# The last norm of a hybrid mixer and expert block: lengths by four tiles, twelve tiles stored whole, the last experts' rows normed behind them

## The chip, the core and the metric

The kernel runs on one core of a Trainium2 chip. The core has five engines that work in parallel, each with its own queue of instructions, which it takes in order: TensorE (PE in the profile, its weight loads PEld), VectorE (DVE), ScalarE (ACT), GpSimd (POOL) and SyncE (SP). Sixteen DMA engines move data between the device's memory (HBM) and the core's SBUF; a transfer is requested by an instruction in the queue of SyncE, ScalarE or GpSimd. The metric is the device time of one execution in microseconds.

## What is computed

The reference is one residual block and a final norm, for 2048 tokens of 1024 numbers in float32. A norm, a projection and two mixers come first (a short convolution and a gated delta rule), then an output projection, then a mixture of 32 experts with two experts to a token, then the norm with which this change deals:

```python
def rms_norm(x, g):
    xf = x.astype(jnp.float32)
    y = xf * lax.rsqrt(jnp.mean(xf * xf, axis=-1, keepdims=True) + EPS)
    return (y * g.astype(jnp.float32)).astype(x.dtype)
...
        x = x + jnp.concatenate([y_a, y_b], axis=-1) @ w_out[l]
        h = rms_norm(x, ffn_norm_g[l]).reshape(Bsz * S, D)
        x = x + hier_moe(h, router_group_w[l], router_expert_w[l], w_gate[l], w_up[l], w_down[l]).reshape(Bsz, S, D)
    return rms_norm(x, final_norm_g)
```

`hier_moe` sends each token to two experts of one group of eight, and adds the two experts' outputs (SwiGLU, 1024 to 512 to 1024), each times a gate.

## The kernel before

The first 1170 us or so are mixers, output projection and router. The sum that goes into the final norm is an accumulator in HBM, `acc_d`, 2048 rows of 4 KB. The output projection writes it tile by tile (a tile is 128 tokens, there are 16).

Then the experts follow as jobs, in an order set by their number of tokens (ranks); the last three of the order, `LAST = 3`, are the ones with the fewest, with places for 120, 116 and 112 tokens (`CAPS`). A job gathers its tokens' rows, turns them (`turn`), multiplies with gate and up (`gate_up`, line 1059), then with down (`down`, lines 1094 to 1103), and an indirect DMA with an add puts the result into the rows of `acc_d` (`add`, line 1072). The weights of the job after the next are read meanwhile into staging buffers of 128 x 1024 (`stage()`, ten of them in two pools) and split into two halves of float16 by ScalarE and VectorE (lines 92 and 93).

The last norm can start before the last experts have ended, since the tokens that these three don't have need nothing more. `bix` holds, for each tile, the row numbers of its 128 tokens, and for a token of one of the last three experts a number past the end, which an indirect DMA skips. `norm_all` (lines 1362 to 1392) works through the sixteen tiles: an indirect read of the rows into a staging buffer (`load`, line 1368), the squares and their sum on ScalarE (`square`, line 1344), mean plus epsilon on VectorE (line 1345), the power of -1/2 on GpSimd (`root`, line 1348; called the root here), the product with root and gain on VectorE (`scale`, line 1351; called the gain here), and an indirect store into the output (line 1385). `AHEAD = 6` tiles are read ahead of the first square. All reads, stores and roots are in GpSimd's queue.

The tokens of the last three experts are normed by themselves, `finish` (line 1407): after an expert's sum, its rows are read from `acc_d` (`rows_of`, line 1396), which waits until that sum has landed, and then squared, rooted, multiplied and stored (`norm_chunk`, line 1404). For the last expert the rows are read before its down product, which is added to them in SBUF (`J.base`, line 1101); they are not written back to `acc_d`.

The kernel is written in Tile: its text gives the order of the instructions as a priority (`weave` takes pieces of several generators in turns; `NA` says how many pieces of the norm go into the two halves of each of the last three jobs), and a planner orders each engine's queue by priority and readiness in its own estimate of time, so it can move a ready instruction forward. It derives all waits from the tiles and tensors that are read and written; `apart` tells it that two accesses of the same tensor touch different rows, so that no wait is drawn.

After the last job stands a loop for tokens beyond an expert's places (line 1493). Its count is zero or more, and the waits for all stores stand at its entry.

Of the kernel before, what the change touches and what calls it, by code (L numbers as in the profile page):

```python
# [38 lines left out]
def hybrid_block(ctx, tc, x, mix_g, w_in, ca_w, ca_g, dn_w, a_log, dt_bias, dn_g, w_out,  # L39
# [13 lines left out]
    # ---------------------------------------------------------------- constants  # L53
# [16 lines left out]
    def weave(*parts):  # L70
        """Traces generators (generator, number of its pieces, begin, end) in turns, by begin and end in a common span."""
        live = [[b + (e - b) * 0.5 / n, (e - b) / n, g] for g, n, b, e in parts if n]
        while live:
            m = min(live, key=lambda o: o[0])
            if next(m[2], 0) == 0:
                live.remove(m)
            m[0] += m[1]
# [21 lines left out]
    # ================================================================ mixers  # L99
    with ExitStack() as ph1:  # L100
# [10 lines left out]
        # weights of beta and alpha: hi | lo  # L111
# [34 lines left out]
        def merge(main, others):  # L146
            """Traces main, 24 pieces of it, with the others spread over it; main may be None."""
# [15 lines left out]
        if True:  # L163
# [16 lines left out]
            # ---- norm of x, its halves, transposed  # L180
# [25 lines left out]
            # ---- beta, decay sums  # L206
            gates = {}

            def gate_cols(b):
# [13 lines left out]
                # sigmoid  # L223
# [5 lines left out]
                # softplus: max(z, 0) + log1p(exp(-|z|))  # L229
# [37 lines left out]
            def stage1(h, b, ws, X):  # L267
# [14 lines left out]
                # causal depthwise convolution, silu  # L282
# [12 lines left out]
                # x * sigmoid(x); beyond e^41 the sigmoid is below every float32 that matters to a sum with 1  # L295
# [14 lines left out]
            def stage2(h, b, X):  # L310
# [5 lines left out]
                # token rows of k and the lengths of k  # L316
# [14 lines left out]
                # decays, with the length of k  # L331
# [18 lines left out]
                # k k', k q'  # L350
# [12 lines left out]
                # inverses of the diagonal blocks of 16, a block to a partition  # L363
# [6 lines left out]
                # token rows of v  # L370
# [24 lines left out]
            def stage3(h, b, X):  # L395
# [4 lines left out]
                # (I - C)^-1 by doubling of the blocks; Tm: the inverse, U: its transpose  # L400
# [6 lines left out]
                # blocks of 16: only the even blocks' columns of the one, the odd blocks' of the other change  # L407
# [17 lines left out]
                # blocks of 32  # L425
# [31 lines left out]
                # the recurrence over the chunks  # L457
# [29 lines left out]
                # norm over the head (the length of q inside), gate, halves  # L487
# [28 lines left out]
            # ---- the short convolution's half  # L516
# [51 lines left out]
            # ---- the first unit: its projections start with the first tile of tokens  # L568
# [55 lines left out]
            # block numbers of row and column  # L624
# [27 lines left out]
            # selectors of the rows of the decays: row r holds part r // 16 of unit r % 16  # L652
# [37 lines left out]
            # ---- from here the space of the delta half serves the output projection  # L690
# [27 lines left out]
    # ================================================================ output projection, router  # L718
    IO = bass.IndirectOffsetOnAxis
    SYNC = mybir.DependencyInfo(mybir.DependencyClass.Sync, mybir.DependencyReason.DATA)  # L720
    NSP = 3                         # experts picked early: the ones with the fewest tokens in the first half
    NST = 2                         # of them in two passes: the first blocks' tokens, the last block's
    C1, C2 = 96, 48
    NE1 = S - TB                    # tokens of the first blocks
    # places of the picked experts, then of the others by their number of tokens
# [3 lines left out]
    LAST = 3                        # experts whose tokens are normed by themselves  # L729
# [15 lines left out]
    # expert weights: (hi, lo), row tile, column; rows of 512 or 1024; the gain of the norm is in gate and up  # L745
# [4 lines left out]
    def stage(pool=None):  # L750
        """A buffer of 128 rows of 1024; when the output projection is through there are more of them."""
# [31 lines left out]
    # router state  # L783
# [28 lines left out]
    # tokens by expert and place, less S: the sums, in SBUF, by place and rank  # L812
# [13 lines left out]
    def first_of(oh, val, shape, n):  # L826
        """oh: one-hot of the first of the zeros of val (at most 0) along the last axis."""
# [6 lines left out]
    def route(b):  # L834
# [30 lines left out]
        # places of the tokens in their experts  # L865
# [13 lines left out]
        # by expert and place (places past the last capacity only go to the blocks of the overflow)  # L879
# [10 lines left out]
        if b >= NB - 2:  # L890
            # the first experts' tokens: places below C1, C2 places from there on
# [7 lines left out]
        # gates 1 / (1 + e^d) / sum, e^d / (1 + e^d) / sum, with d = m[2] = l2 - l1  # L899
# [12 lines left out]
        if b == NB - 2:  # L912
            # the last block's tokens of the first experts stand behind the first C1 places
# [9 lines left out]
    def pick():  # L923
        """The experts with the fewest tokens in the first two blocks: fewer than C1 there, of 32 for 2048."""
# [23 lines left out]
    def entries(w, r, i, src, end, ids):  # L948
        """src: token - S, 0 where there is none."""
# [67 lines left out]
    # ---- an expert's tokens: fetched, gate and up, down  # L1017
    class Job:
        def __init__(self, key, chunks):
            self.key, self.chunks = key, chunks         # chunks: (index, index of the gate, index of the sum, width)  # L1020
            self.n = sum(c[3] for c in chunks)
            self.base = None                            # what the tokens had before
# [62 lines left out]
    def down(J):  # L1085
# [18 lines left out]
        else:  # L1104
            # columns as rows first, turned afterwards
# [35 lines left out]
    # ---- order of the work  # L1141
# [220 lines left out]
    def norm_all():  # L1362
# [15 lines left out]
        for t in range(NT + 2):  # L1378
# [3 lines left out]
            if 1 <= t <= NT:  # L1382
                xs[t - 1].root()
# [143 lines left out]
```

## Time and profile before

| | us |
|---|---|
| median of three runs | 1969.21 |
| lowest and highest run | 1964.92, 1973.45 |
| span of the profiled execution | 1978.5 |
| TensorE busy | 1774.9 (90%) |
| VectorE busy | 1407.2 (71%) |
| ScalarE busy | 1017.3 (51%) |
| GpSimd busy | 476.2 (24%) |

The shares are means over the whole span. The profiled execution took 9.3 us more than the median of the runs; all rows below are of that one execution, and their times count from the start of its span. In a line of a timeline the bracket at the end says how long the engine stood idle before the instruction and what ended that idle time.

### The profile page before, as it was taken

What the parts mean: (1) busy time and instruction counts of PE and PEld (TensorE: products, weight loads), DVE (VectorE), ACT (ScalarE), POOL (GpSimd) and SP (SyncE); (2) the same over time, 40 slices, a digit from 0 to 9 for tenths busy, and PEclk for the clock granted to TensorE, in tenths of its full rate; (3) what the DMA queues carried; (4) which work ended last, traced back from release to release, by engine and by line L of the source; (5) the groups of instructions that cost most, each with busy time, mean ns of one, the idle gap of its engine ahead of it and who ended that gap; (6) DMA issues with size and microseconds to landing.
All of it is one profiled execution on the core that took longest, in us unless ns stands there. A gap on an engine that the chain in (4) does not pass through costs nothing. (4 is left out here: it accounts for less than half of the span.)

```text
span 1978.5 us, 43091 instructions
## 1 busy us (share of the span) xinstructions
PE 1774.9 (90%) x16783; PEld 1218.3 (62%) x16783; DVE 1407.2 (71%) x2756; ACT 1017.3 (51%) x1700; POOL 476.2 (24%) x408
## 2 busy tenths in 40 slices
PE   6789999999999999999999988998889999999820
PEld 5455555555555554444454466888888999999720
DVE  8889888888888745323246748887778888888623
ACT  6654435345344323211334546776667777767522
POOL 1321211121121100000000114333222443443366
PEclk9889999999999999999999998999999999999965
DMA  4222002002001023002357858999999999999853
GB/s 141 66 67 52 10 15 51 10 16 52 9 13 45 25 66 114 27 17 59 130 173 254 294 169 269 336 312 304 290 308 362 347 334 356 341 342 299 281 162 138
DMA packets 203763, 329.25 MB, mean 166 GB/s; under 512 B 45021, under 2 KB 99366, under 8 KB 203554
## 3 DMA queue, kind: packets, MB, share of 16 engines
q1 hardware_dynamic: 177010, 264.90, 39.9%
q0 software_dynamic: 22016, 52.48, 10.3%
q10 hardware_dynamic: 4528, 9.06, 1.2%
q8 instruction: 133, 2.18, 0.5%
q14 instruction: 76, 0.62, 0.1%
HBM read 276.21 MB, written 54.53 MB: 167 GB/s over the span
## 5 line engine op out<-in xcount | busy, mean ns | idle before, releaser
L134 PE MATMUL acc<-hT,whl 128*128 128x512 f16 x2640 | 635.0, 381 | 0.2 <-DVE hT L203 0.2
L1059 PE MATMUL a<-xT,wgu 128*128 128x136 f16 (+19 forms) x6528 | 407.7, 225 | 22.8 <-DVE sl L1066 13.7
L1059 PEld LDWEIGHTS <-wgu 128*128 128x128 f16 x6528 | 399.3, 100 | 30.4 <-issue 25.9
L134 PEld LDWEIGHTS <-whl 128*128 128x128 f16 x2640 | 253.0, 99 | 248.2 <-issue 11.2
L93 DVE SCALAR_TENSOR_TENSOR wgu<-mst,gw,wgu 128x1024 f16<-128x1024 f32 x256 | 317.2, 1277 | 15.8 <-ACT wgu L92 15.8
L92 ACT ACTIVATE wgu<-mst,gw 128x1024 f16<-128x1024 f32 x256 | 279.0, 1138 | 31.3 <-DMA mst<-in_w_up_dram 28.2
L979 PE MATMUL a<-wo,yb 128*128 128x512 f16 x768 | 178.0, 384 | 0.0
L1072 POOL DMA_INDIRECT acc_d<-yo,tabS x53 | 106.0, 1999 | 257.1 <-ACT yo L1120 200.3
L93 DVE SCALAR_TENSOR_TENSOR wd<-mst,wd 128x1024 f16<-128x1024 f32 x128 | 154.5, 1215 | 6.2 <-ACT wd L92 6.2
L1129 PE MATMUL a<-ac,wd 128*128 128x136 f16 (+12 forms) x1920 | 142.8, 230 | 2.7 <-issue 1.2
L92 ACT ACTIVATE wd<-mst 128x1024 f16<-128x1024 f32 x128 | 130.7, 1045 | 19.4 <-DMA mst<-in_w_down_dram 17.3
L1129 PEld LDWEIGHTS <-wd 128*128 128x128 f16 x1920 | 130.2, 98 | 5.7 <-issue 3.9
L979 PEld LDWEIGHTS <-yb 128*128 128x128 f16 x768 | 72.5, 99 | 80.5 <-issue 5.4
L294 DVE SCALAR_TENSOR_TENSOR cv<-raw,pcol,cv 128x512 f32<-128x512 f32 x144 | 114.9, 800 | 1.6
L1028 POOL DMA_INDIRECT xr<-h_d,tabG x54 | 69.5, 1286 | 171.7 <-PE t L1044 161.8
L1066 DVE SCALAR_TENSOR_TENSOR sl<-a,sl 128x136 f32<-128x136 f32 (+19 forms) x136 | 39.6, 293 | 91.4 <-ACT sl L1065 80.5
L1065 ACT ACTIVATE sl<-a 128x136 f32<-128x136 f32 (+19 forms) x136 | 37.1, 275 | 123.9 <-PE a L1059 101.4
L1094 PE MATMUL pl<-wd,ac 128*120 128x512 f16 (+6 forms) x336 | 80.4, 384 | 0.7 <-ACT ac L92 0.7
L382 DVE TENSOR_TENSOR pr<-Ts,fs 32x1 f32<-32x1 f32 (+14 forms) x240 | 76.6, 319 | 4.0 <-DMA fs<-dscr 0.3
L1116 PE MATMUL pl<-id,yt 128*128 128x128 f32 (+13 forms) x320 | 55.4, 293 | 25.4 <-ACT yo L1120 19.5
L1033 POOL DMA_INDIRECT gs<-gt_d,gix x54 | 74.0, 1371 | 16.4 <-issue 16.0
L545 ACT ACTIVATE osq<-acv 128x512 f32<-128x512 f32 x16 | 10.1, 628 | 125.5 <-DVE acv L543 125.5
(351 smaller groups left out, 2592.3 us busy)
## 6 DMA issues: line engine op xcount, KB each, us to landing
mst<-in_w_gate_dram SPq DMA_DIRECT2D x256, 256.0 KB
mst<-in_w_up_dram SPq DMA_DIRECT2D x256, 256.0 KB
mst<-in_w_down_dram SPq DMA_DIRECT2D x128, 512.0 KB
wst<-in_w_in_dram SPq DMA_DIRECT2D x28, 512.0 KB
xt<-in_x_dram SPq DMA_DIRECT2D x16, 512.0 KB
ydr<-yh SPq DMA_DIRECT2D x64, 128.0 KB
x<-in_x_dram SPq DMA_DIRECT2D x16, 512.0 KB
yb<-ydr SPq DMA_DIRECT2D x16, 512.0 KB
```

The costliest lines, as they stand in the source:

```text
L92: A.activation(hi, src, AF.Copy, scale=scale)
L93: (eng or V).scalar_tensor_tensor(lo, src, scale, hi, op0=OP.mult, op1=OP.subtract)
L134: T.matmul(acc, w[:, i, k, :], hT[b][:, j, k, :], start=(n == 0), stop=(n == 3 * KT - 1))
L294: V.scalar_tensor_tensor(y, tap(j), pcol[:, q:q + 1], y, op0=OP.mult, op1=OP.add)
L382: V.tensor_tensor(q, Ts[:, 0:i, 0:i].rearrange("p j m -> p m j"), bc(fs[:, None, 0:i, i], [32, i, i]), op=OP.mult)
L979: T.matmul(po, yb[:, i, k, c * P:(c + 1) * P], wo[:, j, k, n * FF:(n + 1) * FF], start=(q == 0), stop=(q == 3 * KT - 1))
L1028: G.indirect_dma_start(out=xr[0:cw].rearrange("p a k c -> p (a k c)"), out_offset=None, in_=h2_d[0:end, :], in_offset=IO(ap=ix, axis=0))
L1033: G.indirect_dma_start(out=g[0:cw], out_offset=None, in_=gt_d[0:end * NE, :], in_offset=IO(ap=gx, axis=0))
L1059: T.matmul(pg[:, q, 0:n], wq[:, i, k, q, f * P:(f + 1) * P], xT[:, j, k, 0:n], start=(z == 0), stop=(z == 3 * KT - 1))
L1072: st = G.indirect_dma_start(out=acc_d, out_offset=IO(ap=sx, axis=0), in_=yo[0:cw], in_offset=None, bounds_check=S - 1, oob_is_err=False, c ...
L1094: T.matmul(py[0:n], ac[:, i, k, 0:n], wd[:, j, k, q * FF:(q + 1) * FF], start=(z == 0), stop=(z == 3 * FF // P - 1))
L1129: T.matmul(pg[:, u, 0:n], wd[:, i, k, d * P:(d + 1) * P], ac[:, j, k, 0:n], start=(z == 0), stop=(z == 3 * FF // P - 1))
```

## The change

Three things change, all behind line 1332.

The norm of the tiles goes by groups of four. Four squares write their sums into four columns of one tile, one instruction on VectorE and one root on GpSimd do the four columns, and four gains follow, each with its store behind it. `AHEAD` is 8, and `NA` spreads the pieces anew.

The stores of tiles 0 to 11 (`NPL = 12`) are plain DMAs of 128 whole rows on SyncE's queue. They also write rows of the last experts' tokens, whose contents in the staging buffer are left over from before; these rows are stored again later. Tiles 12 to 15 keep the indirect store that skips them.

The last experts' rows are read once, in the last job: after the sums of the two experts before have landed, three indirect reads get the rows of the last expert (`J.base`) and of the two before (`ends`, into buffers of the pool `o1`). The two are normed and stored behind the store of tile 12; the last expert's rows are written to `acc_d` by an indirect DMA (in `finish`), normed into another buffer and stored at the end. The indirect stores are declared apart from one another where their rows differ, the plain stores from none of them.

The rest of the diff takes out comments and is left out here.

```diff
@@ -1332,32 +1332,28 @@
             for _ in g:
                 pass
 
-    class Norm:
-        def __init__(self, xf, n):
-            self.x, self.n = xf[0:n], n
-        def square(self):
-            self.s = o2.tile([P, 1], F32, name="ss4", bufs=6)[0:self.n]
-            jk = m2.tile([P, D], F16, name="jk", tag="yt")
-            A.activation(jk[0:self.n], self.x, AF.Square, accum_out=self.s)
-            V.tensor_scalar(self.s, self.s, 1.0 / D, EPS, op0=OP.mult, op1=OP.add)
-        def root(self):
-            G.tensor_tensor(self.s, self.s, mhalf[0:self.n, 0:1], op=OP.pow)
-        def scale(self):
-            V.scalar_tensor_tensor(self.x, self.x, self.s, gfin[0:self.n], op0=OP.mult, op1=OP.mult)
-    AHEAD = 6
+    AHEAD = 8
     LP, WE = 0, 0.6
-    NA = ((0, 3), (6, 6), (9, 9))
+    NA = ((0, 4), (12, 10), (10, 10))
+    GT = 4
+    NPL = NT - GT
     loads, stores, adds, outs = [], [], [], []
 
     def apart(st, others):
         for o in others:
             tc.declare_no_dep(st.ins, o.ins, reason="rows of other tokens")
+    def square(x, s, n=P):
+        jk = m2.tile([P, D], F16, name="jk", tag="yt")
+        A.activation(jk[0:n], x, AF.Square, accum_out=s)
+    def root(s):
+        V.tensor_scalar(s, s, 1.0 / D, EPS, op0=OP.mult, op1=OP.add)
+        G.tensor_tensor(s, s, mhalf[0:s.shape[0], 0:s.shape[1]], op=OP.pow)
+    def gain(x, s, n=P, dst=None):
+        V.scalar_tensor_tensor(x if dst is None else dst, x, s, gfin[0:n], op0=OP.mult, op1=OP.mult)
 
     def norm_all():
         xs = {}
@@ -1375,52 +1371,70 @@
         for t in range(AHEAD):
             load(t)
             yield 1
-        for t in range(NT + 2):
-            if t < NT:
-                xs[t] = Norm(xs[t], P)
-                xs[t].square()
-            if 1 <= t <= NT:
-                xs[t - 1].root()
-            if t >= 2:
-                st = G.indirect_dma_start(out=out2, out_offset=IO(ap=bix[:, t - 2:t - 1], axis=0), in_=xs.pop(t - 2).x,
-                                          in_offset=None, bounds_check=S - 1, oob_is_err=False)
-                apart(st, outs + stores)
-                stores.append(st)
-                load(t - 2 + AHEAD)
-            if 1 <= t <= NT:
-                xs[t - 1].scale()
+        for t0 in range(0, NT, GT):
+            s = o2.tile([P, GT], F32, name="ss4")
+            for i in range(GT):
+                square(xs[t0 + i], s[:, i:i + 1])
+                yield 1
+            root(s)
+            for i in range(GT):
+                t = t0 + i
+                x = xs.pop(t)
+                gain(x, s[:, i:i + 1])
+                if t < NPL:
+                    nc.sync.dma_start(out2[t * P:(t + 1) * P, :], x)
+                else:
+                    st = G.indirect_dma_start(out=out2, out_offset=IO(ap=bix[:, t:t + 1], axis=0), in_=x,
+                                              in_offset=None, bounds_check=S - 1, oob_is_err=False)
+                    apart(st, outs + stores)
+                    stores.append(st)
+                load(t + AHEAD)
+                yield 1
+    def rows_of(ix, cw, xf):
+        G.indirect_dma_start(out=xf[0:cw], out_offset=None, in_=acc_d, in_offset=IO(ap=ix, axis=0))
+        return xf[0:cw]
+    def norm_rows(x, dst=None):
+        n = x.shape[0]
+        s = o2.tile([P, 1], F32, name="ss1", bufs=4)[0:n]
+        square(x, s, n)
+        root(s)
+        gain(x, s, n, dst)
+    def store_rows(x, sx, more=True):
+        st = G.indirect_dma_start(out=out2, out_offset=IO(ap=sx, axis=0), in_=x, in_offset=None,
+                                  bounds_check=S - 1, oob_is_err=False)
+        if more:
+            apart(st, stores)
+            outs.append(st)
+    def finish(J):
+        if J.base:
+            ix, gx, sx, cw = J.chunks[0]
+            st = G.indirect_dma_start(out=acc_d, out_offset=IO(ap=sx, axis=0), in_=J.base[0][0:cw], in_offset=None,
+                                      bounds_check=S - 1, oob_is_err=False)
+        else:
+            st = add(J)[0]
+        apart(st, loads)
+        adds.append(st)
+        yield 1
+    def last_rows(na, ends):
+        for _ in na:
+            if len(stores) == 1 and not outs:
+                for x, sx in ends:
+                    norm_rows(x)
+                for x, sx in ends:
+                    store_rows(x, sx)
             yield 1
 
-    def rows_of(ix, cw):
-        xf = stage()
-        G.indirect_dma_start(out=xf[0:cw], out_offset=None, in_=acc_d, in_offset=IO(ap=ix, axis=0))
-        return xf
-    def norm_chunk(xf, sx, cw):
-        N = Norm(xf, cw)
-        N.square()
-        N.root()
-        N.scale()
-        return G.indirect_dma_start(out=out2, out_offset=IO(ap=sx, axis=0), in_=xf[0:cw], in_offset=None,
-                                    bounds_check=S - 1, oob_is_err=False)
-    def finish(J):
-        ix, gx, sx, cw = J.chunks[0]
-        if not J.base:
-            st = add(J)[0]
-            apart(st, loads)
-            adds.append(st)
-            yield 1
-        st = norm_chunk(J.base[0] if J.base else rows_of(ix, cw), sx, cw)
-        apart(st, stores)
-        outs.append(st)
-        yield 1
     eids = {}
 
     def part(j, i):
         if j < NST or j >= len(jobs):
             return
         r = jobs[j].key
@@ -1471,7 +1485,10 @@
         if left <= LAST:
             n1, n2 = NA[LAST - left]
             if left == 1:
-                J.base = [rows_of(J.chunks[0][0], J.n)]
+                J.base = [rows_of(J.chunks[0][0], J.n, stage())]
+                ends = [(rows_of(L.chunks[0][0], L.n, o1.tile([P, D], F32, name="end", tag="hh")), L.chunks[0][2])
+                        for L in jobs[-LAST:-1]]
+                na = last_rows(na, ends)
             parts.append((slices(na, n1), n1, 0, 1))
         weave(*parts)
         parts = [(prio(part(j + 2, 0), PW if j == 0 else 0), 4, 0, 1) if left != 3 else (seq(*(part(j + 2, i) for i in range(3))), 12, 0, WE)]
@@ -1487,8 +1504,11 @@
             parts.append((slices(na, n2), n2, WE if left == 3 else 0, 1))
         weave(*parts)
     drain(na)
+    end = stage()[0:J.n]
+    norm_rows(J.base[0][0:J.n], end)
+    store_rows(end, J.chunks[0][2])
     nb_ = nc.values_load(nblk[0:1, 0:1], min_val=0, max_val=NB2)
     with tc.For_i(0, nb_, 1) as i:
         overflow()
@@ -1498,7 +1518,9 @@
         J = Job("o", [(ox[:, 1:2], ox[:, 2:3], ox[:, 0:1], P)])
         drain(fetch(J), load_expert("o", e), turn(J), gate_up(J), down(J))
         add(J)
-        norm_chunk(rows_of(ox[:, 1:2], P), ox[:, 0:1], P)
+        x = rows_of(ox[:, 1:2], P, stage())
+        norm_rows(x)
+        store_rows(x, ox[:, 0:1], False)
 
 
 # ---- launch: one core; inputs and outputs as the reference has them ----
```

## Rows read from the trace of the kernel before

**Rows 1.** Windows by stretch of 1850 to 1980: PE, PEld, DVE, ACT, POOL, clock, DMA share, GB/s.

```profile
1850.00:1900.00 50.00, 34.99 (x488) 30.17 (x486) 28.30 (x47) 26.81 (x49) 33.37 (x22) 0.87 0.64 211
1900.00:1950.00 50.00, 6.36 (x35) 3.71 (x32) 11.75 (x20) 9.27 (x20) 30.57 (x25) 0.60 0.51 153
1950.00:1980.00 30.00, 0.00 (x0) 0.00 (x0) 8.00 (x9) 3.18 (x6) 14.91 (x13) 0.50 0.33 120
```

**Rows 2.** Timelines of PE and ACT: start, us, line, operation, count, idle before, releaser.

```profile
1896.34 4.63 PE L1059 MATMUL a<-xT,wgu 128*128 128x112 f16 x48 [11.46 <-DVE sl L1066]
...
1903.56 3.44 PE L1094 MATMUL pl<-wd,ac 128*112 128x512 f16 x15 [0.65 <-ACT ac L92]
...
1880.85 1.06 ACT L1344 ACTIVATE jk<-mst 120x1024 f16<-120x1024 f32 x1 [9.25 <-DMA mst<-acc_d,tabG]
...
1930.50 1.06 ACT L1344 ACTIVATE jk<-mst 116x1024 f16<-116x1024 f32 x1 [26.99 <-DMA mst<-acc_d,tabG]
```

**Rows 3.** Timeline of POOL, 1857 to 1967: reads, stores, roots of the last norm.

```profile
1857.51 1.86 POOL L1368 DMA_INDIRECT mst<-acc_d,bix  x1 [12.42 <-DMA mst<-in_w_down_dram]
...
1862.29 6.33 POOL L1368 DMA_INDIRECT mst<-acc_d,bix  x1 [0.57 <-DVE wgu L93]
...
1885.04 2.07 POOL L1368 DMA_INDIRECT mst<-acc_d,bix  x1 [0.18 <-issue]
...
1889.25 2.04 POOL L1385 DMA_INDIRECT out_dram<-mst,bix  x1 [0.18 <-issue]
...
1905.54 2.15 POOL L1072 DMA_INDIRECT acc_d<-yo,tabS  x1 [0.30 <-issue]
...
1920.36 1.30 POOL L1396 DMA_INDIRECT mst<-acc_d,tabG  x1 [8.48 <-DMA acc_d<-yo,tabS]
...
1923.30 1.04 POOL L1368 DMA_INDIRECT mst<-acc_d,bix  x1 [0.30 <-issue]
...
1931.99 0.57 POOL L1348 TENSOR_TENSOR ss<-ss,mhalf 116x1 f32<-116x1 f32 x1 [6.41 <-DVE ss L1345]
...
1966.91 0.99 POOL L1404 DMA_INDIRECT out_dram<-mst,tabS  x1 [1.61 <-DVEq L1493]
```

**Rows 4.** Windows of the tail, columns as in group 1 (DMA share, then GB/s, last).

```profile
1866.00:1869.00 3.00, 1.00 (x20) 1.00 (x20) 3.00 (x8) 0.55 (x3) 2.69 (x2) 1.00 0.00 0
...
1869.00:1887.00 18.00, 14.54 (x200) 11.86 (x198) 4.64 (x13) 7.22 (x15) 11.68 (x10) 1.00 0.72 203
...
1872.00:1884.00 12.00, 10.66 (x148) 8.68 (x147) 1.08 (x3) 3.15 (x7) 6.25 (x7) 1.00 0.88 260
...
1869.00:1971.00 102.00, 24.56 (x272) 19.23 (x269) 30.74 (x54) 24.41 (x52) 68.76 (x56) 0.64 0.53 168
...
1971.00:1978.50 7.50, 0.00 (x0) 0.00 (x0) 0.00 (x0) 0.00 (x0) 0.00 (x0) 0.50 0.00 0
```

**Rows 5.** Groups by shape, 1840 to 1980: count, busy us, mean ns, idle before, releasers.

```profile
L1385 POOL DMA_INDIRECT out_dram<-mst,bix x16 | 29.4, 1836 | 3.3 <-issue 3.3
...
L1351 DVE SCALAR_TENSOR_TENSOR mst<-mst,ss,gfin 128x1024 f32<-128x1024 f32 x16 | 20.6, 1285 | 23.6 <-POOL ss L1348 20.8 <-DMA mst<-acc_d,bix 2.8
L1344 ACT ACTIVATE jk<-mst 128x1024 f16<-128x1024 f32 x16 | 16.7, 1044 | 13.3 <-DMA mst<-acc_d,bix 13.3
L1348 POOL TENSOR_TENSOR ss<-ss,mhalf 128x1 f32<-128x1 f32 x16 | 12.8, 800 | 1.3 <-DVE ss L1345 0.9
...
L1072 POOL DMA_INDIRECT acc_d<-yo,tabS x4 | 6.7, 1684 | 15.6 <-ACT yo L1120 14.7 <-issue 0.9
```

**Rows 6.** Timelines of SyncE's queue and of DVE, same columns as group 2.

```profile
1856.07 0.33 SPq L775 DMA_DIRECT2D mst<-in_w_down_dram  x1
...
1863.13 4.62 DVE L93 SCALAR_TENSOR_TENSOR wd<-mst,wd 128x1024 f16<-128x1024 f32 x4
...
1889.10 1.29 DVE L1351 SCALAR_TENSOR_TENSOR mst<-mst,ss,gfin 128x1024 f32<-128x1024 f32 x1 [2.75 <-POOL ss L1348]
```

**Rows 7.** DMA queues, 1840 to 1980: packets, MB, share of 16 engines.

```profile
q0 software_dynamic: 6912, 18.46, 42.6%
```

## Prediction: what the change does to the time

> **What bounds the kernel now.** I read the windows of the last 130 us first, then the timeline of TensorE and ScalarE, then GpSimd's timeline, then the groups of instructions by shape, and last the transfers. The windows show that the change lies in a tail of its own: from 1850 on TensorE's busy time falls from 35.0 us in a stretch of 50 to 6.4 and then to nothing, while GpSimd is busy 33.4, 30.6 and 14.9 us [rows 1]. The last matmul ends at 1903.56 + 3.44 = 1907.0 [rows 2], and the span ends 71.5 us later. What runs there is the last norm: sixteen reads of a tile, sixteen norms, sixteen stores, and a read, norm and store for each of the last three experts.
>
> GpSimd paces it. It issues every read and every store and computes every root, in a queue that goes in order. From the first tile store at 1889.25 to the last store at 1966.91 [rows 3] it alternates root and store with hardly an idle moment, except for two holes. The first is 8.48 us ahead of the read at 1920.36, which waits for the sum of expert 30 to land; that sum was issued at 1905.54, took 2.15, and landed 12.7 us after. The second is 6.41 us ahead of the root at 1931.99, which waits for those rows to be squared [rows 3]. ScalarE stood 26.99 us for these rows, with tiles behind it in its queue [rows 2]. The transfer engines are no limit on average: share 0.53 and 168 GB/s from 1869 to 1971; then nothing moves, and 7.5 us of closing follow [rows 4].
>
> **The change, part by part.** The profiled execution has a span of 1978.5 us; the median of the runs is 1969.2, so a result on the span is multiplied by 0.995 at the end.
>
> Twelve stores leave GpSimd. One is 1.836 us, with 3.3 / 16 = 0.21 us of issue around it [rows 5]: 12 x 2.04 = 24.5 us. They become plain stores on SyncE's queue, which has no weights left to ask for by then. Issue there is 0.33 us in the nearest row, the last weight request [rows 6], hidden beside the gain that makes the next tile (1.285 us, [rows 5]); without that cover it would be 12 x 0.33 = 4 us.
>
> Sixteen roots of one column become four of four columns. One takes 0.800 us [rows 5]. A root of four columns has no row; it lies between 0.8 (nothing for width) and 3.2 (four times). I take 0.8, because the cost of a root in these rows follows the instruction, not its one column per partition: 12 x 0.8 = 9.6 us off GpSimd, or 0 at the other end. The twelve small products on VectorE that go with them are free, since VectorE is busy only 30.7 of 102 us [rows 4].
>
> The group has a price at its start: the first gain waits for four squares in place of one, 3 x 1.04 = 3.1 us [rows 5]. It also has a credit: the first square no longer stands behind the rows of expert 29 in ScalarE's queue (that square came at 1880.85 [rows 2], while tile reads had been issued from 1857.5 on [rows 3]). I put the two together at 0, between -5 and +3.
>
> The second hole goes, 6.4 us: the rows of experts 29 and 30 are now read together with the last one's and squared behind the tiles, when they have long landed. The first hole stays, at another place: the three reads still wait for the sum of expert 30, and what is queued behind them on GpSimd (the roots of the later groups, the reads of the last tiles) waits too. Eight tiles read ahead in place of six give that wait more work in front of it. I leave it at its price of now.
>
> Added on GpSimd: one write of the last expert's sum into the accumulator, 1.684 us as the other writes there [rows 5] plus 0.3 issue, 2.0 us; nothing if the engine waits for something else then, 4 us if it waits for the reads before it.
>
> A new wait: the scattered stores of tiles 12 to 15 and those of the last experts' rows write the same output as the twelve plain stores and are not declared apart from them, so the store of tile 12 waits for the landing of the store of tile 11. Behind it on GpSimd stand the roots and stores of the last experts' rows, the stores of tiles 13 to 15, the write and the last norm. From below its price is 3.1 us: the last store's issue ends at 1967.9 and transfers are over by 1971 [rows 3, 4]. From above it is the 12.7 us of the sum that landed behind a backlog. I take 5, near the first, because the plain stores do not queue behind reads on GpSimd's queue.
>
> Sum on GpSimd: -24.5 - 9.6 - 6.4 + 2.0 + 5.0 = -33.5 us; with all terms at their worse ends (-24.5 + 4 - 0 - 6.4 + 4 + 12.7 + 3) it is -7, with all at their better ends (-24.5 - 9.6 - 6.4 + 0 + 3.1 - 5) -42.
>
> **What is late next: the transfers.** From 1869 to 1971 they moved 102 us x 168 GB/s = 17.1 MB in 0.53 x 102 = 54 us of full use [rows 4]. Whole tiles carry the last experts' rows too (120 + 116 + 112 = 348 rows of 2048, twelve sixteenths of it, 4 KB each: 1.1 MB), and the new write is 0.46 MB; 18.6 MB then, of a software queue that moved 18.46 MB in the tail [rows 7], or 59 us of full use. Starting at 1869 that ends at 1928 at a share of 1, at 1936 at the share of 0.88 that the engines reach while reads stand in line (1872 to 1884), at 1951 at the 0.72 of 1869 to 1887, which has an idle stretch in it [rows 4]. GpSimd's sum would need 1971 - 33.5 = 1937.5, so a share of 0.86 throughout, and the new landing waits speak against that. I take 0.78, between the two rows: 59 / 0.78 = 75.6 us, to 1944.6, which is 26.4 us earlier. Closing stays at 7.5. Span 1952, and in terms of the median 1969.2 - 26.3 = 1943.
>
> [...]
>
> **The rivals.**
> First, VectorE holds GpSimd up in bursts. A store that runs while a gain runs takes 2.04 us (1889.25, with the gain at 1889.10), a read with no gain beside it 1.04 (1923.30) [rows 3, 6]. Under four conversions of weights back to back (4.62 us from 1863.13) one read took 6.33, and no byte moved from 1866 to 1869 [rows 3, 4, 6]. Four gains back to back are 4 x 1.285 = 5.1 us; if each of the four bursts holds the queue as a whole, 20.5 us of the sum go: -33.5 + 20.5 = -13, time 1956. For it: that one read. Against: reads from 1857.5 on went through under conversions too, the first at 1.86 [rows 3]. [...]
>
> Second, the reading of the last rows gets in the way. If the planner puts these three reads ahead of the root of the third group, that group and the fourth wait for a landing of 12.7 us and for three reads of 1.3 us [rows 3]: -26.4 + 12.7 + 4 = -9.7, time 1959.6. Then the change does not do what it says, "behind the tiles". For it: the reads come first in the text of the last job. Against: eight tiles ahead, and the planner has lifted ready reads before (nine tile reads, from 1857.51 to 1885.04, before the first tile store [rows 3]).
>
> Third, slower: the transfers keep the pace of now, because each is started by the landing of another. 18.6 MB at 168 GB/s are 110.7 us, to 1979.7 instead of 1971: +8.7, time 1978. It decides from a mean pace under 18.6 / 102 = 182 GB/s. For it: plain and scattered stores would share the engines and waits for landings are added. Against: 260 GB/s from 1872 to 1884 and gaps without any transfer that are GpSimd's doing [rows 4].
>
> Fourth, better: the transfers come near full use and all terms to their better ends, -40: 1929.
>
> **How the numbers follow.** Forecast 1943 (its own range 1935 to 1952) 0.60; bursts, 1956, 0.16; reads in the way, 1960, 0.08; slower, 1978, 0.08; better, 1929, 0.08. Half a per cent, 10 us, is about what a measurement of this kernel tells from no change. Faster by more: 0.58 + 0.14 + 0.02 + 0.08, some 0.80 with the tails; within: 0.12; slower: 0.08. The range 1928 to 1962 leaves out the slower case and the half of the better one, and the ends of the others, 0.17 in all.
>
> **What would show it right or wrong.** Right: GpSimd with 4 scattered tile stores, 4 wide roots under 1 us, no hole of 6 us ahead of a root; SyncE with 12 stores; transfers at a share near 0.78 from 1869 on, over by 1945. The wait before tile 12's store shows the price of the landing. Bursts: reads of over 4 us beside four gains. Reads in the way: GpSimd idle over 8 us at a read of the accumulator with roots behind it. Wrong altogether: TensorE's last matmul later than 1907, because products of the last expert stand behind four gains on VectorE; it stood 11.46 us for VectorE now [rows 2]. That would hit the last norm, which needs the last expert's product.

## The result and the profile after

The changed kernel takes 1949.2 us as the median, the kernel before 1971.0 in the same comparison: a ratio of 0.9892, interval 0.9868 to 0.9915, or 21 us less. The forecast was 1943 with a range of 1928 to 1962, so the direction and roughly the size are right; why they are is another matter, since several terms of the sum and the step on the transfers were wrong, and their errors partly cancel.

The two profiled executions have spans of 1978.5 and 1946.2 us, 32 us apart. Eleven of these lie ahead of the tail, where the change has nothing: the first tile read starts at 1857.51 before [rows 3] and at 1846.74 after. From that read to the end it is 121.0 us before and 99.5 after, 21.5 less, and this agrees with the medians. All stages below are counted from the first tile read of the same execution.

GpSimd's timeline of the kernel after, with the columns as before (start, duration, operation, idle time before it and its releaser), shows the stages:

```profile
1846.74 1.87 POOL L1364 DMA_INDIRECT mst<-acc_d,bix  x1 [12.36 <-DMA mst<-in_w_down_dram]
...
1884.35 2.14 POOL L1072 DMA_INDIRECT acc_d<-yo,tabS  x1 [1.69 <-ACT yo L1103]
...
1900.55 0.94 POOL L1395 DMA_INDIRECT mst<-acc_d,tabG  x1 [11.39 <-issue]
1901.79 1.00 POOL L1395 DMA_INDIRECT end<-acc_d,tabG  x1 [0.30 <-issue]
1903.10 1.25 POOL L1395 DMA_INDIRECT end<-acc_d,tabG  x1 [0.30 <-issue]
1904.36 2.04 POOL L1353 TENSOR_TENSOR ss<-ss,mhalf 128x4 f32<-128x4 f32 x2
1911.92 0.56 POOL L1353 TENSOR_TENSOR ss<-ss,mhalf 120x1 f32<-120x1 f32 x1 [5.52 <-DVE ss L1352]
1915.29 1.55 POOL L1353 TENSOR_TENSOR ss<-ss,mhalf 116x1 f32<-116x1 f32 x1 [2.81 <-DVE ss L1352]
1918.74 1.05 POOL L1387 DMA_INDIRECT out_dram<-mst,bix  x1 [1.90 <-SPq L1513]
...
1925.55 1.29 POOL L1406 DMA_INDIRECT out_dram<-end,tabS  x1 [0.84 <-DMA out_dram<-end,tabS]
...
1935.20 0.98 POOL L1406 DMA_INDIRECT out_dram<-mst,tabS  x1 [5.21 <-DMA out_dram<-end,tabS]
```

The unbroken row of roots and stores of [rows 3] is gone: 4 stores of tiles are left on this queue, and they come at the very end. What the reader is to see instead is idle time. The longest stands ahead of the three reads at 1900.55: they wait for the sum of expert 30, issued at 1884.35 (the profile names no releaser on this line; in the runs "half" and "later" below it names that sum on the same read). Behind them stand the roots of the third and fourth group (1904.36); the third group's squares were done by 1886.8. Two more idle stretches, 5.52 and 2.81 us, stand ahead of the roots of the last experts' rows (1911.92 and 1915.29). The last store waits 5.21 us for the landing of the store of expert 30's rows, issued at 1925.55.

The windows of the kernel after (PE, PEld, DVE, ACT, POOL, clock, DMA share, GB/s) show the same from the side of the transfers, to be read beside [rows 4]:

```profile
1875.00:1887.00 12.00, 9.84 (x176) 8.94 (x173) 5.41 (x8) 6.24 (x13) 8.13 (x7) 1.00 1.01 388
...
1893.00:1902.00 9.00, 1.93 (x8) 0.87 (x6) 0.06 (x1) 1.09 (x3) 1.15 (x2) 0.88 0.18 49
...
1858.20:1939.20 81.00, 28.15 (x273) 19.23 (x269) 29.06 (x43) 22.94 (x50) 39.04 (x33) 0.70 0.69 227
...
1939.00:1946.20 7.20, 0.00 (x0) 0.00 (x0) 0.00 (x0) 0.00 (x0) 0.00 (x0) 0.50 0.00 1
```

While reads and plain stores overlap, the engines are full at 388 GB/s. Then, for nine microseconds in which GpSimd waits for one sum, they run at a share of 0.18.

### The profile page after: what moved, and what is told of

It is laid out like the page before. It is cut to its first block, busy times and chain, and to the rows that moved or that the text cites. A ratio compares the mean times of both kernels' runs of the same rounds, so it can differ in the third digit from the quotient of the medians.

```text
span 1946.2 us, 43064 instructions
## 1 busy us (share of the span) xinstructions
PE 1771.7 (91%) x16783; PEld 1211.5 (62%) x16783; DVE 1406.6 (72%) x2744; ACT 1017.4 (52%) x1700; POOL 448.7 (23%) x385
## 5 line engine op out<-in xcount | busy, mean ns | idle before, releaser
L134 PEld LDWEIGHTS <-whl 128*128 128x128 f16 x2640 | 253.2, 99 | 249.8 <-issue 13.3
L1059 PE MATMUL a<-xT,wgu 128*128 128x136 f16 (+19 forms) x6528 | 396.8, 223 | 3.1 <-DVE sl L1066 2.2
L1059 PEld LDWEIGHTS <-wgu 128*128 128x128 f16 x6528 | 390.5, 98 | 8.6 <-issue 4.1
L1094 PE MATMUL pl<-wd,ac 128*120 128x512 f16 (+6 forms) x336 | 87.0, 406 | 21.5 <-ACT ac L92 21.5
```

What stands on the lines that cost most here:

```text
L134: T.matmul(acc, w[:, i, k, :], hT[b][:, j, k, :], start=(n == 0), stop=(n == 3 * KT - 1))
L1059: T.matmul(pg[:, q, 0:n], wq[:, i, k, q, f * P:(f + 1) * P], xT[:, j, k, 0:n], start=(z == 0), stop=(z == 3 * KT - 1))
L1094: T.matmul(py[0:n], ac[:, i, k, 0:n], wd[:, j, k, q * FF:(q + 1) * FF], start=(z == 0), stop=(z == 3 * FF // P - 1))
```

## The experiments

I cut the tail into three stages with marks that every kernel has: from the first tile read to the issue of expert 30's sum; from there to the first read of the last experts' rows, which waits for its landing; from there to the end. The middle stage is the landing itself only where the profile names it as what ended the wait; in "scatter", "cap120" and "scatter120" it names something else, and in the changed kernel and "groupsonly" nothing, so there it is an upper bound. Times in us, of one profiled execution each; the ratio to the kernel before with its interval comes from timed rounds.

| kernel | to the sum | landing | rest | tail | ratio to before |
|---|---|---|---|---|---|
| before | 48.0 | 14.8 | 58.1 | 121.0 | 1 |
| changed | 37.6 | 16.2 | 45.7 | 99.5 | 0.9892 (0.9868 to 0.9915) |
| scatter | 44.3 | 16.3 | 51.7 | 112.3 | 0.9946 (0.9930 to 0.9961) |
| rowsonly | 51.5 | 15.2 | 48.0 | 114.6 | 0.9946 (0.9927 to 0.9965) |
| groupsonly | 52.3 | 15.2 | 49.2 | 116.7 | 0.9969 (0.9956 to 0.9983) |
| half | 35.7 | 17.1 | 43.8 | 96.6 | 0.9889 (0.9868 to 0.9911) |
| later | 37.6 | 14.6 | 44.7 | 96.9 | 0.9890 (0.9869 to 0.9911) |
| latesq | 30.0 | 15.3 | 56.9 | 102.2 | 0.9912 (0.9891 to 0.9932) |
| before120 | 48.7 | 6.8 | 54.4 | 109.9 | 0.9905 (0.9888 to 0.9922) |
| cap120 | 36.4 | 9.9 | 39.4 | 85.7 | 0.9795 (0.9774 to 0.9816) |
| cap117 | 37.0 | 10.3 | 40.1 | 87.4 | 0.9805 (0.9783 to 0.9828) |
| scatter120 | 45.9 | 9.5 | 45.3 | 100.7 | 0.9882 (0.9857 to 0.9907) |
| capall | 37.0 | 10.5 | 41.2 | 88.7 | 0.9704 (0.9682 to 0.9726) |
| best | 36.6 | 9.8 | 44.8 | 91.2 | 0.9730 (0.9709 to 0.9751) |

**The parts of the change.** My theory was that GpSimd's queue sets the tail; the rival, that the transfers do. First, the changed kernel with all stores given back to GpSimd ("scatter"):

```diff
-    NPL = NT - GT
+    NPL = 0
...
-            if len(stores) == 1 and not outs:
+            if len(stores) == NT - GT + 1 and not outs:
```

> The changed kernel with all sixteen tiles stored by indirect DMAs from GpSimd (none by SyncE); groups of four and the late reading of the last rows stay. If GpSimd's queue sets the tail: twelve stores of 2.04 us come back to it, 24.5 us, less the 1.9 to 5 us of waiting for plain stores to land that goes; some of it can fall into the 11.4 us in which the queue stands for the sum of expert 30. So 8 to 20 us more than the changed kernel's 1949, 1957 to 1969, and over 95 us from the first tile read to the end becoming 108 to 119. If transfers set it: 1.1 MB fewer, 3 to 5 us less, 1944 to 1946.

Measured: 0.9946 / 0.9892 is 0.55% or 10.7 us more than the changed kernel (1959.9 against 1949.2). The direction is the queue's, against the transfers, which would have gained; the size is at the lower end of what the queue let one expect. The run does not separate the time of the stores in the queue from what their landings hold up: in "scatter" the wait ahead of the three reads ends with the landing of a scattered store.

Then also a root for each tile ("rowsonly"), so that the late reading of the last rows is left, together with the eight tiles read ahead and the new spread of the pieces (`AHEAD`, `NA`), which stay in every run made from the changed kernel:

```diff
-        for t0 in range(0, NT, GT):
-            s = o2.tile([P, GT], F32, name="ss4")
-            for i in range(GT):
+        for t0 in range(0, NT, 1):
+            s = o2.tile([P, GT], F32, name="ss4", bufs=6)
+            for i in range(1):
                 square(xs[t0 + i], s[:, i:i + 1])
                 yield 1
-            root(s)
-            for i in range(GT):
+            root(s[:, 0:1])
+            for i in range(1):
```

> The late reading of the last experts' rows alone: all tiles stored from GpSimd, a root for each tile. If GpSimd's queue sets the tail: as the run with scattered stores, plus twelve roots of 0.8 us, 9.6 us, less 3 us for the first gain that waits for one square in place of four: 1964 to 1976, that is within 0.3% of the kernel before. If the removed hole ahead of the last experts' root (6.4 us) is a gain by itself, 1964. If transfers set it: 1946 to 1949.

Measured: the same 0.9946 as "scatter". That is 1960 us, a little under what the theory and the rival of the removed hole gave and far above what the transfers gave. The roots in groups are worth nothing here that the intervals (3 to 4 us to either side) could tell, and the late reading with `AHEAD` and `NA` is worth 10.6 us; no run has those two alone, so what they give by themselves is not shown. GpSimd's groups by shape of these two kernels, 1840 to the end, say what the groups did on the queue (count, busy us, mean ns); rowsonly first, then scatter:

```profile
L1387 POOL DMA_INDIRECT out_dram<-mst,bix x16 | 17.1, 1067 | 8.0 <-issue 3.8 <-DVE ac L93 3.6 <-DVE mst L1356 0.3
L1353 POOL TENSOR_TENSOR ss<-ss,mhalf 128x1 f32<-128x1 f32 x16 | 12.1, 762 | 1.7 <-DVE ss L1352 1.5
```

```profile
L1387 POOL DMA_INDIRECT out_dram<-mst,bix x16 | 24.3, 1522 | 9.8 <-DVE mst L1356 6.5 <-issue 2.6 <-DVE ss L1352 0.3
...
L1353 POOL TENSOR_TENSOR ss<-ss,mhalf 128x4 f32<-128x4 f32 x4 | 4.2, 1043 | 0.1
```

Four wide roots take 4.2 us where sixteen took 12.1: 8 us less. But the stores cost 7.2 us more in total, and the saving is gone. One store shows it best, in GpSimd's timeline of "scatter":

```profile
1915.61 5.41 POOL L1387 DMA_INDIRECT out_dram<-mst,bix  x1 [2.20 <-DVE mst L1356]
```

Beside it, in VectorE's timeline of the same kernel, stand the gains:

```profile
1914.04 6.06 DVE L1356 SCALAR_TENSOR_TENSOR mst<-mst,ss,gfin 128x1024 f32<-128x1024 f32 x5
```

The store's 5.41 us end at 1921.0, just behind the five gains, which end at 1920.1; the next store takes 0.99. This is the rival of the bursts, and it is real, but it is shown only where a store stands in GpSimd's queue beside them. The plain stores of the changed kernel don't: their twelve requests on SyncE's queue take 0.33 us in the median and 0.81 at most, and the four behind the start of a burst of five gains (1905.72 to 1911.78) 0.33 to 0.64.

The groups without the late reading ("groupsonly", with all stores on GpSimd) keep the last experts' rows behind each sum:

```diff
...
+        x = J.base[0][0:cw] if J.base else rows_of(ix, cw, stage())
+        norm_rows(x)
+        store_rows(x, sx)
+        yield 1
...
-                na = last_rows(na, ends)
...
-    end = stage()[0:J.n]
-    norm_rows(J.base[0][0:J.n], end)
-    store_rows(end, J.chunks[0][2])
```

> The groups of four alone (with eight tiles read ahead): all tiles stored from GpSimd, the last experts' rows read, normed and stored behind each expert's sum as before. If GpSimd's queue sets the tail: 9.6 us of roots less than the kernel before, 3 us more for four squares at the start: 1961 to 1968. If the order on ScalarE sets it (its squares wait for rows with the experts' products behind them): 1968 to 1975, no gain or a loss, since more squares stand ahead.

Measured: 0.9969, 6.1 us less than before (1964.5 in its median), as the queue let one expect. So the gains of the parts seem to depend on what else is there: groups, again with `AHEAD` and `NA`, 6 us by themselves and nothing to be told from noise on top of the late reading.

**The bytes.** The plain stores with half of their columns ("half"):

```diff
-                    nc.sync.dma_start(out2[t * P:(t + 1) * P, :], x)
+                    nc.sync.dma_start(out2[t * P:(t + 1) * P, 0:D // 2], x[:, 0:D // 2])
```

> The changed kernel, but each plain store of tiles 0 to 11 writes only the first 512 of 1024 columns (the other half of these rows is left out): 3.1 MB less to transfer, the same number of instructions. If transfers set the tail: 3.1 MB at the 227 GB/s of the tail are 13.8 us less, 1935. If the queues and single landings set it: the landing of the last plain store and of reads beside stores comes 1 to 4 us sooner, 1945 to 1949.

Measured: 0.9889 against 0.9892, no difference, though 3.1 MB less moved. The sum of expert 30 lands as late as ever, as GpSimd's timeline of "half" says:

```profile
1899.38 0.95 POOL L1395 DMA_INDIRECT mst<-acc_d,tabG  x1 [12.32 <-DMA acc_d<-yo,tabS]
```

So the transfers do not set the tail by what they carry, and the step of the prediction that let them do so falls.

**The order.** Two edits ask what stands in the way of what. "later" makes the three reads of the last job after the first half of its work instead of ahead of it:

```diff
-            if left == 1:
-                J.base = [rows_of(J.chunks[0][0], J.n, stage())]
...
         weave(*parts)
+        if left == 1:
+            J.base = [rows_of(J.chunks[0][0], J.n, stage())]
...
```

> The changed kernel with the three reads of the last experts' rows moved behind the first half of the last job, so that the root of the third group stands ahead of them in GpSimd's queue (that of the fourth still behind). If the reads in the way of the roots cost time: the third group's gains and plain stores go at 1887 in place of 1906 and the store of tile 12 no longer waits for them: 4 to 8 us less, 1941 to 1945. If the sum of expert 30 sets the tail whatever stands behind it: 1947 to 1950.

Measured: 0.9890, no difference. The third group's root now comes ahead of the reads, 15 us sooner counted from the first tile read, and the end does not move: the landing still ends the wait. "latesq" moves squares behind expert 30's products:

```diff
-    NA = ((0, 4), (12, 10), (10, 10))
+    NA = ((0, 4), (4, 18), (10, 10))
```

> The changed kernel with eight pieces of the tiles' norm moved from the first half of the last job but one to its second half (4 and 18 pieces in place of 12 and 10), so that fewer squares stand ahead of expert 30's products on ScalarE. If ScalarE's squares, which wait for rows, hold up expert 30's sum: that sum is issued 5 to 10 us sooner than 1884 (counted from the first tile read: 28 to 33 us in place of 37.6) and the time falls by 4 to 8 us. If GpSimd or the landing sets it: 1947 to 1955, with the tiles' stores later.

Measured: the sum of expert 30 is issued 7.6 us sooner (30.0 for 37.6), as expected if ScalarE's squares hold it up, but the time does not fall: 0.9912. What was gained ahead of the sum is lost behind it (56.9 for 45.7). The tiles' own squares come later (the last of them at 1914.65, 64.4 us from the first tile read, and in the changed kernel at 1902.11, 55.4 us), which fits the second expectation.

**The landing.** In every kernel so far the sum of expert 30 took 14.6 to 17.1 us from issue to landing, whether half the bytes were moved beside it or not; the sum of expert 29 took 6.7 in the kernel before (issued at 1868.92, the read behind it at 1875.61). One has 116 rows, the other 120, and the share of 0.18 in the last nine microseconds is that of about 3 engines out of 16 (0.18 x 16 = 2.9); in the kernel before it is 0.20 from 1917.0 to the read at 1920.36. The new theory, an estimate from such shares, was that the transfer of 116 rows runs on some 4 engines and one of 120 rows on more; the rival, that it stands in line. "cap120" gives that expert four places more:

```diff
-            132, 132, 128, 128, 124, 124, 124, 120, 120, 120, 116, 112]
+            132, 132, 128, 128, 124, 124, 124, 120, 120, 120, 120, 112]
```

> The changed kernel with 120 places in place of 116 for the last expert but one (expert 30 of the order), so that its sum, its reads and its stores are transfers of 120 rows. [...] Then the sum of expert 30 lands in 6 to 9 us, its rows in 6 in place of 10.8, and the time falls by 8 to 14 us to 1935 to 1941. Rival: the sum lands late because it stands behind reads and stores in line; 120 rows change nothing, 1947 to 1951, and the wait stays at 15 us or more.

Measured: 1927.9 and 0.9795, 19 to 21 us less than the changed kernel, more than the theory asked for. GpSimd's timeline of "cap120":

```profile
1815.77 0.96 POOL L1028 DMA_INDIRECT xr<-h_d,tabG  x1 [5.80 <-PE t L1044]
...
1840.49 1.87 POOL L1364 DMA_INDIRECT mst<-acc_d,bix  x1 [8.98 <-DMA mst<-in_w_gate_dram]
...
1876.90 1.65 POOL L1072 DMA_INDIRECT acc_d<-yo,tabS  x1 [0.65 <-ACT yo L1103]
...
1886.80 0.93 POOL L1395 DMA_INDIRECT mst<-acc_d,tabG  x1 [5.62 <-DVE ac L93]
...
1915.43 0.98 POOL L1406 DMA_INDIRECT out_dram<-mst,tabS  x1 [1.61 <-DVE mst L1356]
```

The landing takes 9.9 us in place of 16.2, the last store waits 1.61 for its gain and no longer for a store of 116 rows, and the tail is 13.8 us shorter. Another 7.5 lie just ahead of it: from the gather of expert 30's tokens (1815.77) to the first tile read it is 24.7 us here and 32.2 after (from 1814.51; the gather itself came 1.3 us later here). It is so in the others too: 31.3 in the kernel before, 24.7 to 25.0 in "before120", "cap117" and "capall". ScalarE waits for weights there in the changed kernel (3.56 us at 1823.15) and hardly at all in "cap120". That would fit a gather of 116 rows that is slow as well, with weights waiting behind it; but the engines are full in both stretches (shares 1.01 and 1.04), and no run separates this, so the cause of these 7.5 us stays open.

The same edit in the kernel before ("before120"):

> The kernel before with 120 places in place of 116 for expert 30. If 116 rows run on 4 engines: the hole of 8.5 us ahead of the read and that of 6.4 us ahead of the root of expert 30's rows shrink by 5 to 8 and 2 to 4 us: 7 to 11 us less, 1960 to 1964. Rival, backlog: no change, 1967 to 1973.

Measured: 0.9905, 19 us less, where 7 to 11 were expected; the landing is 6.8 us in place of 14.8, and the tail is 11.1 us shorter. The rest lies ahead of the tail, for which the expectation had no term. To tell the number 116 itself from what else came with four places more, one place more ("cap117"). Were it the number itself, nearly all of what 120 places gave was due, 1927 to 1934; were it something else, 1940 to 1950:

> The changed kernel with 117 places in place of 116 for expert 30. [...]

Measured: 0.9805, within the interval of 120 places, with a landing of 10.3 us. One row more makes the kernel 17 us faster, so it is not that fewer rows are moved; what sets 116 apart from 117 and 120 no run shows. The windows of the last 8 us ahead of the read, "cap117" first and then "cap120", stand against the share of 0.18 above:

```profile
1889.77:1897.77 8.00, 3.98 (x11) 1.92 (x12) 1.43 (x6) 3.38 (x11) 1.68 (x3) 0.79 0.87 287
```

```profile
1878.60:1886.80 8.20, 2.93 (x7) 1.56 (x8) 1.44 (x6) 4.30 (x11) 2.04 (x2) 0.63 0.93 300
```

Their shares are 0.87 and 0.93, or some 14 and 15 engines of 16 (0.87 x 16 = 13.9). The packets of the changed kernel's trace fit its 0.18: from 1892.7 to its read 2 to 6 are under way at once, mostly 3 or 4. So the slow landing is that of a transfer of which few packets move at a time, with two tile reads finishing beside it. The profile does not name the engines one by one, so on how many of them each of the three transfers ran is not shown.

With the landing out of the way, what are the plain stores worth ("scatter120": scatter with 120 places)?

> All tiles stored from GpSimd, as in the run with scattered stores, with 120 places for expert 30. That run lost 10.7 us against the changed kernel. If part of its stores lay in the hole in which GpSimd waits for the sum of expert 30 (11.4 us with 116 places, 5.6 with 120): the loss grows to 13 to 18 us, 1941 to 1946. If the stores' own price is what was lost (1.0 to 1.5 us each where no gain runs beside them, in place of 2.0): the loss stays at 9 to 12, 1937 to 1940.

Measured: 0.9882 / 0.9795, 0.9% or 17 us more than "cap120", where it was 10.7 with 116 places. Both have an interval of 5 to 7 us to either side, so that the loss grew is not shown. Nor do the stages show stores that had lain in the hole ahead of the three reads: two stand there in either kernel (1893.64 and 1896.34 in "scatter", 1893.89 and 1896.56 in "scatter120"), and the tails differ by 15.0 us here and by 12.8 with 116 places.

Three experts in the middle have 124 places, so their gathers and sums are transfers of 124 rows. "capall" gives them 128, and expert 30 the 120 of "cap120":

```diff
-            132, 132, 128, 128, 124, 124, 124, 120, 120, 120, 116, 112]
+            132, 132, 128, 128, 128, 128, 128, 120, 120, 120, 120, 112]
```

> [...] If such a transfer takes 5 to 8 us from a stretch in which the engines are full with weights, as the gather of 116 rows did (7.5 us from its issue to the first tile read): 10 to 24 us less than with 120 alone (1928), 1904 to 1918. If only the tail is touched by it: 1926 to 1930.

Measured: 0.9704, another 0.9% or 18 us, and the tail is no shorter than with 120 alone (88.7 us and 85.7). It is gained among the weights: from one gather of tokens (1315.61 in "cap120", 1323.95 in "capall") to the thirteenth behind it (1533.13 and 1519.42) it is 22 us shorter. What a single transfer of 124 rows takes of this is not shown. This version beats both kernels, by 3.0% and 1.9%. "later" on top of it is "best":

> The last with the three reads of the last experts' rows behind the third group's root. If the reads stand in the way only as long as the sum of expert 30 lands late: no change to the last, within 3 us. If the third group's 5 us of gains and the landing of its stores were the next to be late: 3 to 6 us less than the last.

Measured: 0.9730, and so neither of the two expectations. In the same rounds the lowest of five runs of "best" (1924.5) lies above the highest of five of "capall" (1922.9), a loss of 7 us between the medians. In the profiled executions 4.7 of this stand ahead of the first gather of an expert's tokens, where the edit does nothing (1127.22 and 1122.54), and 2.5 in the tail; the cause is not shown.

## Why the prediction was right or wrong

Split by the three stages, the 21.5 us of the tail are 10.4 up to the sum of expert 30 (48.0 to 37.6), -1.4 in its landing, and 12.5 behind it (58.1 to 45.7).

*GpSimd paces the tail*: half right. Giving the queue its stores back costs 10.7 us and halving the bytes nothing, so for the stores it is the queue, or what waits in it, and not the bytes that the change relieved. But the longest single wait was for a landing, which the prediction saw as the "first hole" and let stand at its price.

*Twelve stores, -24.5*: mis-sized. They are worth 10.7 us on top of the rest, and 17 by the medians of the kernels with a short landing. The reading of 1.836 us was that of stores beside gains [rows 5]; sixteen stores in "rowsonly" took 1.067 each. And a part of the time that they leave in the queue stands idle: ahead of the roots of the last experts' rows GpSimd waits 5.52 and 2.81 us in the kernel after, while in "scatter" stores fill the queue up to these roots.

*Roots, -9.6*: the four-column root takes 1.05 us, near the lower bound, as chosen. Between "rowsonly" and "scatter" GpSimd saved 8 us in roots and spent 7 more in stores, and the time gained nothing that can be told from noise. That the bursts of gains which come with the groups hold up stores is shown for the store of 5.41 us; for the rest of the 7 us it is argued.

*The second hole, -6.4, the write, +2.0*: the late reading with `AHEAD` and `NA` gave 10.6, more than the 4.4 of these two terms. Its third stage is 10 us shorter than before (48.0 for 58.1) and its first 3.5 longer, and nothing in the runs splits that further. In the changed kernel the hole did not go. The rows were to be squared when they had long landed; they are read only at 1901.79 and 1903.10, behind the sum of expert 30, ScalarE waits 4.41 and 4.9 us for them, and 5.52 and 2.81 us stand ahead of their roots.

*The first hole stays*: it grew, from 8.48 [rows 3] to 11.39 us, with the roots of two groups behind it. That is the second rival, which I gave 0.08 and a time of 1960. It happened, and for the third group it cost nothing: with its root ahead of the reads ("later") the time is the same. The fourth group's root could hardly have come sooner: of its tile reads, one issued by 1888.16 landed only at 1900.9, about when the sum of expert 30 did, and its last square ended at 1903.2.

*The new wait, +5*: the store of tile 12 waited 1.90 us, less than the lower bound, since the queue stood for expert 30's rows until shortly before. Another wait had no term: the last store behind the landing of the store of expert 30's rows, 5.21 us, of which 3.9 come after its gain was done (1931.30); the kernel with 120 places waits 1.61 us there, for the gain alone.

*The transfers are late next, share 0.78*: the step that failed. 18.4 MB moved (81.0 us x 227 GB/s; 18.6 were estimated), at a share of 0.69 and not 0.78, so that they were over 81 us after the mark instead of 75.6. The share was low because requests waited for landings, not because the engines were at a limit, and "half" shows that bytes do not count. What stood in the place of the bytes was the landing of one sum of 116 rows at a share of 0.18, worth 13.8 us of the tail in "cap120", for which the prediction had only the 8.48 us of the first hole that stays. The forecast came near in part by luck: GpSimd's sum of 33.5 us was 12 too large against the 21.5 measured, and the step on the transfers, wrong in its reason, took 7.1 of them off again.

*TensorE later than 1907 would make it wrong altogether*: its last matmul did come later, at 1907.8, which is 61.1 us from the first tile read and was 49.5 before. ScalarE held it up, not VectorE: its idle time for tile reads is 26.5 us in the tail, with the products of experts 30 and 31 behind it. TensorE's timeline of the kernel after shows two of these waits, 4.28 and 8.56 us for the activation in line 92:

```profile
1890.48 4.45 PE L1094 MATMUL pl<-wd,ac 128*112 128x512 f16 x13 [4.28 <-ACT ac L92]
1903.49 4.33 PE L1094 MATMUL pl<-wd,ac 128*112 128x512 f16 x11 [8.56 <-ACT ac L92]
```

The second of them lies behind the square at 1900.91, which had waited 8.16 us for the late tile read. VectorE came in as well, one step later: the second half of the last product's add (line 1101) runs at 1921.12, behind gains, 13.3 us after that matmul's end. It did not hurt the last norm, whose rows had to be read behind the landing at 1900.55 anyway, whose root stands behind stores in GpSimd's queue until 1929.39, and whose store had 5.21 us to wait. What it costs with a short landing was not tried apart.

## What to carry to other kernels

Look at the share of the DMA engines while everybody waits for one transfer: here it was 0.18 with a transfer of 116 rows, 0.87 with one row more, and the kernel 17 us faster, so the number of rows is the first thing to try. A queue's busy time is worth what it takes from the path; time that falls into a wait which stays is not won. Price an instruction by rows in which its neighbours are those that it will have.

## What was not expected of the hardware

The sum of expert 30 lands 6 to 8 us later with 116 rows than with 117 or 120 (14.6 to 17.1 us against 6.8 to 10.5). Giving three experts in the middle 128 places for 124 took off another 18 us. A store from GpSimd beside a burst of five gains took 5.41 us ("scatter"); the next one, behind the burst, 0.99.
